# The last pair of heads in layer A: queries, keys and values turned by VectorE and moved through DRAM, and layer A's output product in another order of tiles

## The chip, the core and the metric

The kernel runs on one core of a Trainium2 chip. A core has five engines with instruction streams of their own: TensorE (PE) multiplies matrices into PSUM, which has eight banks; VectorE (DVE), ScalarE (ACT) and GpSimd (POOL) work elementwise; SyncE (SP) issues the DMAs of this kernel. They are ordered only by semaphores. The metric is the time of one execution on the device in microseconds (us), the median of several.

## The reference

Two layers on 512 tokens of width 1024, all in float32. Layer A attends within dilated windows of three kinds, and merges the three by the denominators of their softmaxes. Layer B attends within neighbourhoods of a grid of 8 x 64 tokens. Cut to layer A:

```python
def mixer_a(hn, w_in, w_out, q_gain, k_gain, t5_bias):
    proj = hn @ w_in
    ...
    for g, (window, dilation) in enumerate(((128, 1), (512, 4), (2048, 16))):
        q = rms_norm(qkv[:, :, g, 0], q_gain[g])
        k = rms_norm(qkv[:, :, g, 1], k_gain[g])
        o, lse = dilated_group_attention(q, k, v, t5_bias[...], dilation, reach)
        ...
    alpha = jax.nn.softmax(jnp.stack(lses), axis=0)
    y = jnp.sum(alpha[..., None] * jnp.stack(outs), axis=0)
    y = y.reshape(b, s, BRANCH_WIDTH).astype(hn.dtype) * jax.nn.silu(gate)
    return y @ w_out

def reference(x, ...):
    for i in range(DEPTH):
        hn = rms_norm(x, norm_gain[i])
        y = mixer_a(hn, ...) if i % 2 == 0 else mixer_b(hn, ...)
        x = x + y
```

There are 16 heads of 64 columns. The kernel takes them as eight pairs (`hc` 0 to 7) of 128 columns.

## The kernel before

**Products.** A float32 operand is held as a high and a low part, and each product of two 128-wide tiles is three matmuls (`mm3`, line 243, recorded at line 237). `splits` (line 188) makes both parts of a weight: ScalarE casts the high part (line 141), VectorE or GpSimd subtracts it to get the low part (line 149). The weights come in pieces of at most 1024 columns (`wraw`, line 201), three pieces ahead of their use; of the halves made from them, up to four wait for PE.

**Stages of layer A.** For each pair `main_a` (line 661) runs the projection of keys of the far groups, their values, and queries with the near key (`project_qk`, keys `rawk` and `rawq`), 32 steps each, then the near values (`v0_a`) and the gate (`gate_a`), 8 steps each. For the last pair the order is: `rawq`, `rawk`, the gate of pair 6, values, gate. Behind it comes the output product (`out_product`, line 1126), in which eight tiles of 128 output columns are added up over the eight pairs' y. Its first four tiles go over pairs 0 to 6 (28 steps), then three more tiles over pairs 0 to 6 (21 steps), then all seven take pair 7, and the eighth tile goes over all pairs.

**Between the projections.** The side work of a pair is: norm of queries and keys (`head_norm`, scaled at line 335), scores and softmax (`attn_a`), turning of the probabilities, and their weighting of the values (`weigh`, then `put_y`). The scores need queries and keys with the head's columns on the partitions, so both have to be transposed. Pairs 0 to 6 do this without PE: VectorE turns blocks of 32 x 32 in place (`turn_raw`, line 588, recorded at 592), a DMA writes the whole tile of 1536 KB to DRAM (`qd`, line 722), four DMAs of 384 KB read the blocks back in the places they belong to (`qt`, line 729), and ScalarE copies them into four areas (`split_q`, lines 777 and 791). Near values take the same way (`move_v`: `vd`, `vv`, then a copy into `v0`), and so do the probabilities (`turner`: `td`, `pt`).

Pair 7 uses PE instead: `q_a` and `k_a` transpose six groups of four tiles of 128 x 128 by PE (`transpose4`, recorded at line 241) into PSUM, from where ScalarE and VectorE copy them (lines 705, 708, 712, 680); `v_a` does one such group with the values. Its probabilities are transposed by PE too, in eight groups (`turn_p`, line 1007); these are outside the change.

**What sets the order.** PE runs in the order in which the program emits its instructions. That order comes from a planner: `run` (line 1092) walks through the steps of `main` and, between them, through the `side` work. Its clock counts PE work in units of its own (`matmul`, line 233): three matmuls of 512 columns are 640 units, a transpose 109. `later_on(delay, job)` puts a job on this clock; `yield "wait", key, delay` puts the side work off until a stamp's time plus a delay; `yield 600` puts it off by that much; a bare `yield` by the next of a cycle (500, 500, 700 for the last pair). `yield key, "turned"` in the output product makes the main work wait until the side has set that stamp, and the planner then emits side work until it has. The other engines are ordered by a scheduler that works with a simulated timeline, except for instructions under `tc.keep_in_program_order`. All engines and the DMA issue on SP take their instructions strictly in that order, so a waiting one holds up those behind it.

**PSUM.** Four banks hold the tiles that are being added up (`acc`), four are shared by scores (four at a time), transposes, weighting (two) and the later tiles of the output product (`acc2`).

**Around the last pair before.** Its scores of the first half wait for the stamp of its own gate; they come two steps into the output product. The weighting of pair 6 follows, then transposes of probabilities, the second half's scores, their transposes, and the values' group. Only then "turned" is stamped and the last weighting is emitted, after the 28th step; three `acc2` tiles follow. The bias of a pair (`bias_a`, five DMAs) is loaded 26,000 units after the start of its projections.

Of the kernel before, what the change touches and what calls it, by code (L numbers as in the profile page):

```python
# [22 lines left out]
P = 128  # L23
# [9 lines left out]
LINE = 384 + 2 * 448  # L33
W5 = 5 * 32
RUN = 6 * 64
EB = 8 * W5

# [15 lines left out]
OUTS = {  # L53
    A_OUT: ((512, 7), (384, 7), (512, 1), (384, 1), (128, 8)),
    B_OUT: ((512, 6), (256, 6), (512, 1), (256, 1), (128, 7), (512, 1), (384, 1), (128, 8)),
# [4 lines left out]
def tile_hybrid_encoder(  # L60
# [457 lines left out]

    moved = lambda hc: hc < NHC - 1

    def part(n):
        return rk[:, 1024 * n : 1024 * n + 1024].rearrange("p (i c) -> p i c", i=4)

    def project_qk(n, ns, key, hc, guard, first=False, **kw):

        box = []
        blocked = key == "raw" or (moved(hc) and key in FS)

        def evac(i, acc):
            if not box:  # L530
                if blocked:
                    box.append(key)
                elif key == "rawk":
                    box.append(rq[:, 2048:3072].rearrange("p (i c) -> p i c", i=4))
                elif key == "v":
                    box.append(rk[:, 4 * n * hc : 4 * n * hc + 4 * n].rearrange("p (i c) -> p i c", i=4))
                else:
                    box.append(rq[:, : 4 * n].rearrange("p (i c) -> p i c", i=4))
                if key == "rawk":
                    st["v12", hc] = part(hc % 3)  # L540
                box.append(None if key == "v" else wk.tile([P, 32], F32, tag="ss", name="ss"))
            raw, ss = box
            if blocked:
# [12 lines left out]
            if not first and key != "v":  # L556
                v = blocks_of(i, key + "0" * (key == "raw")) if blocked else raw[:, i, : ns * 64]
                squares(v, ss, i, ns, key == "rawq" and moved(hc))

# [22 lines left out]
    def normed(raw, ss, ns, key, hc):  # L582
        delay = 11000 if key == "rawk" and 0 < hc < NHC - 1 else 0
        head_norm(raw, ss, ns, delay, key == "rawk" and hc == NHC - 1, then=partial(turn_raw, key) if moved(hc) else None)
        st[key, hc] = raw
        stamp[key, hc] = clock[0]
# [36 lines left out]
    def v0_a(hc):  # L623
        acc = []
        yield from project_t(acc)
        yield "v", hc - 1
        vt = vv[:, :S]
        rows = lambda t, a, b: trj(t)[:, a:b]
        for a, b, to in ((0, 28, 4), (28, 32, 0)):
            src = to_trj(acc[0])[:, a:b]  # L630
            nc.vector.tensor_mul(rows(vt, to, to + b - a), src, rows(rs_half, a, b))
        if hc < NHC - 1:
            move_v(hc, vt)
        st["vt", hc] = vt
        stamp["vt", hc] = clock[0]
# [36 lines left out]

    def k_a(hc):
        yield "wait", ("rawk", hc), 12000
        qt = q_tiles(hc)[0]
        raw = st.pop(("rawk", hc))
        for g in range(2):
            tp = transpose4(raw, g * P)
            dst = qt[:, :, 4 + g, :].rearrange("p t (j r) -> p t j r", j=4)
            nc.vector.tensor_scalar(dst, to_tjr(tp), gk[:, g + 1 : g + 2], None, op0=ALU.mult)  # L680
            yield

    def q_tiles(hc):
# [9 lines left out]
    def q_a(hc):  # L693

        yield "wait", ("rawq", hc), 8000 if moved(hc) else 30500
        raw = st.pop(("rawq", hc))
        if moved(hc):
            move_q(hc)
            return
        qt, k0 = q_tiles(hc)  # L700

        by_t = lambda to: qt[:, :, to, :].rearrange("p t (x r) -> p x t r", x=16)
        of_t = lambda tp: tp.rearrange("p (x t r) -> p x t r", x=16, t=4)
        tp = transpose4(raw, 0)
        nc.scalar.copy(by_t(0), of_t(tp))
        yield
        tp = transpose4(raw, 3 * P)
        scaled(trj(k0[:, 64:EXT]), to_trj(tp), 0)
        yield
        for g in range(2):  # L710
            tp = transpose4(raw, (g + 1) * P)
            nc.vector.tensor_copy(by_t(1 + g), of_t(tp))
            yield
        stamp["q", hc] = 0

    def move_q(hc):
# [17 lines left out]
        def land():  # L734
            for a in (0, 2, 1, 3):
                later_on(6500 if hc < NHC - 2 else 5000, partial(read, a))
            yield "wait", ("rawk" if hc < NHC - 2 else "rawq", hc + 1), 0
            assert not left[0]
            split_q(hc, *q_tiles(hc))
            yield  # L740
# [27 lines left out]
    def split_q(hc, qt, k0):  # L768
# [3 lines left out]
        both = slot(hc, "q12", F32)  # L772
        areas = st["areas", hc] = slot(KT - 1, "q0", F32)[:, :S], both[:, :S], both[:, S:]
        for g, to in enumerate(areas):
            src = qt[:, :, g, :].rearrange("p s (x r) -> p s x r", r=8)
            dst = to.rearrange("p (x s r) -> p s x r", s=4, r=8)
            tc.keep_in_program_order(scaled(dst, src, g) if g else nc.scalar.copy(dst, src))

    def v_a(hc):

        yield "wait", ("vt", hc), 2500
        vt = st.pop(("vt", hc))
        tp = bank("tp")
        for i in range(4):
            transpose(tp[:, i * P : (i + 1) * P], vt[:, i * P : (i + 1) * P])
        nc.scalar.mul(v0[hc % 2], tp.rearrange("p (i c) -> p i c", i=4), 2.0)
        stamp["v", hc] = 0
        yield

# [142 lines left out]
    def attn_a(hc):  # L932
# [192 lines left out]

    def out_product(key, sink, late, more):

# [45 lines left out]
        if more == 3:  # L1173
            for k in range(KT):
                yield from step(k, (7,))
            return
# [159 lines left out]
    def main():  # L1336
        for hc in range(NHC):
            if hc:
                later_on(26000, lambda hc=hc: st.__setitem__(("e", hc), bias_a(hc)))
            yield from main_a(hc)  # L1340
        yield from out_product("ya", sink_a, 1, 3)
        gap[0] = cycle((500, 500, 800))
# [8 lines left out]
        for kind, i in B_PARTS:  # L1351
# [4 lines left out]
            else:  # L1356
                yield from gate_b(i)
        yield from out_product("yb", sink_b, 2, 2)

    def side():  # L1360
# [22 lines left out]
        for hc in range(NHC):  # L1383
# [84 lines left out]
def _layout(x, norm_gain, a_w_in, a_w_out, a_q_gain, a_k_gain, t5_bias,  # L1468
# [5 lines left out]

    def outs(w, late, more):
        k, m = KT - late, 512 + P * more
        blk = [w[:k, :, :512], w[:k, :, 512:m]]
        if more == 2:
            blk += [w[k : k + 1, :, :512], w[k : k + 1, :, 512:m], w[: KT - 1, :, 768:896]]
        blk += [w[KT - 1 :, :, :512], w[KT - 1 :, :, 512:896], w[:, :, 896:]]  # L1480
        return [b.transpose(1, 0, 2).reshape(P, -1) for b in blk]
# [6 lines left out]
    for hc in range(NHC):  # L1488
# [4 lines left out]
        parts.append(cols(wa, [9 * D + P * hc]))  # L1493
    parts += outs(wao, 1, 3)
    for kind, i in B_PARTS:
# [6 lines left out]
        parts.append(cols(wb, starts))  # L1502
    parts += outs(wbo, 2, 2)
    w = np.concatenate(parts, axis=1)
# [35 lines left out]
```

## Time and profile before

| | us |
|---|---|
| median of 3 runs | 800.97 |
| lowest, highest | 800.83, 800.97 |
| the profiled execution | 802.38 |
| its span, first to last instruction | 800.6 |
| busy: PE, DVE, ACT, POOL | 795.9, 526.8, 442.3, 222.2 |

The granted clock of TensorE is 1.00 throughout. The durations used below come from the one profiled execution, whose own time is 1.4 us above the median of the runs; between its span and its time lie 1.8 us. In the tables a row names the source line, the engine, the operation, and output<-inputs by the names of tiles; `x` is the count.

### The profile page before, as it was taken

The page shows a single profiled execution, that of the slowest core. Times are in us where ns is not written, and L with a number is a line of the kernel's source. Part 1 is how long each engine was busy: PE and PEld are TensorE (multiplying, and loading weights), DVE is VectorE, ACT ScalarE, POOL GpSimd, SP SyncE. Part 2 cuts the span into 40 slices and gives each one's busy share as a digit, 9 for nine tenths or more (in the row PEclk, how much of TensorE's full clock was granted, in tenths as well). Part 3 has the DMA queues.
Part 4 walks back from the last instruction along what each step waited for, and adds up shares of the span by engine and source line. Part 5 has one row for each costly group of instructions (what it writes and reads, how often), then busy time and mean ns, then how long its engine had stood idle before and what let it go on. Part 6 is the DMA issues. An engine that isn't in the chain of part 4 may idle for free.

```text
span 800.6 us, 17757 instructions
## 1 busy us (share of the span) xinstructions
PE 795.9 (99%) x6718; PEld 653.9 (82%) x6718; DVE 526.8 (66%) x1409; ACT 442.3 (55%) x933; POOL 222.2 (28%) x351
## 2 busy tenths in 40 slices
PE   9999999999999999999999999999999999999998
PEld 7888888888888888888888878888888888887887
DVE  7474575677577467568468568538655878896744
ACT  7442744745744754654664575636336666656721
POOL 2242532441432532432432331211220305020010
PEclk9999999999999999999999999999999999999999
DMA  8578587877977976986987966166646796899464
GB/s 293 159 206 260 162 246 213 262 204 228 297 219 212 280 236 206 275 289 198 264 259 232 267 201 186 31 208 214 167 151 202 204 245 213 207 263 292 147 156 175
DMA packets 97526, 174.76 MB, mean 218 GB/s; under 512 B 16608, under 2 KB 52592, under 8 KB 97440
## 3 DMA queue, kind: packets, MB, share of 16 engines
q1 hardware_dynamic: 97296, 173.36, 74.4%
q8 instruction: 53, 0.87, 0.5%
q14 instruction: 33, 0.27, 0.1%
q10 hardware_dynamic: 144, 0.26, 0.1%
HBM read 130.98 MB, written 50.86 MB: 227 GB/s over the span
## 4 chain that ended last, share of the span: by engine, by line
PE 90%; DVE 5%; DMA 3%; ACT 2%; issue 1%; ACTq 0%; SPq 0%
PE acc L237 79%; PE log L237 4%; PE o L237 4%; DMA vv<-vd 1%; DVE rawq L335 1%; DMA bd<-rawq 1%; PE tp L241 1%; DVE wl L149 1%; DMA wraw<-in_w 1%; PE busy L401 1%; ACT wh L141 0%; ACT p L1300 0%; DVE na L128 0%; ACT p L1305 0%; DVE rawq L592 0%
## 5 line engine op out<-in xcount | busy, mean ns | idle before, releaser
L237 PE MATMUL acc<-wh,hn_h 128*128 128x512 f32 x704 | 277.5, 395 | 0.0
L237 PE MATMUL acc<-wl,hn_h 128*128 128x512 f32 x704 | 273.7, 389 | 0.0
L237 PE MATMUL acc<-wh,hn_l 128*128 128x512 f32 x704 | 273.7, 389 | 0.0
L141 ACT CAST wh<-wraw 128x512 fp32r<-128x512 f32 (+1 forms) x258 | 157.7, 614 | 196.6 <-PE acc L237 168.4
L149 DVE TENSOR_TENSOR wl<-wraw,wh 128x512 fp32r<-128x512 f32 (+2 forms) x187 | 137.6, 737 | 151.4 <-ACT wh L141 149.6
L149 POOL TENSOR_TENSOR wl<-wraw,wh 128x512 fp32r<-128x512 f32 (+1 forms) x72 | 96.3, 1338 | 230.0 <-ACT wh L141 176.4
L237 PEld LDWEIGHTS acc<-wh,hn_h 128*128 128x128 f32 x704 | 132.4, 188 | 31.5 <-issue 3.8
L237 PEld LDWEIGHTS acc<-wh,hn_l 128*128 128x128 f32 x704 | 132.1, 188 | 27.9
L237 PEld LDWEIGHTS acc<-wl,hn_h 128*128 128x128 f32 x704 | 132.2, 188 | 26.8 <-POOL wl L149 0.3
L315 POOL TENSOR_TENSOR sq<-rawq 128x256 f32<-128x256 f32 (+1 forms) x82 | 59.4, 733 | 125.4 <-ACT rawq L555 112.7
L237 PE MATMUL acc<-y,wh 128*128 128x512 f32 (+1 forms) x272 | 81.5, 383 | 0.0
L1003 ACT ACTIVATE p<-p,mn 128x512 f32<-128x512 f32 (+1 forms) x64 | 44.8, 701 | 59.9 <-DVE mn L992 59.9
L237 PE MATMUL acc<-hn_h,wh 128*128 128x512 f32 x192 | 75.9, 395 | 0.1
L237 PE MATMUL acc<-hn_h,wl 128*128 128x512 f32 x192 | 74.8, 390 | 0.0
L237 PE MATMUL acc<-hn_l,wh 128*128 128x512 f32 x192 | 74.8, 390 | 0.0
L316 DVE TENSOR_REDUCE ss<-sq 128x4 f32<-128x256 f32 (+1 forms) x96 | 47.6, 506 | 32.5 <-POOL sq L315 32.1
L237 PEld LDWEIGHTS acc<-y,wh 128*128 128x128 f32 x272 | 48.8, 188 | 9.2 <-issue 0.7
L237 PE MATMUL acc<-y,wl 128*128 128x512 f32 (+1 forms) x136 | 51.4, 378 | 0.0
L335 DVE TENSOR_TENSOR rawq<-rawq,rs 128x256 f32<-128x256 f32 (+1 forms) x96 | 47.0, 550 | 2.5 <-POOL rs L133 2.2
L911 DVE STREAM_TRANSPOSE tr<-p 128x512 f32<-128x512 f32 x56 | 38.9, 706 | 11.6 <-ACT p L827 11.4
L555 ACT ACTIVATE rawq<-acc,rs_n 128x512 f32<-128x512 f32 (+1 forms) x76 | 46.1, 613 | 0.5
L827 ACT ACTIVATE p<-p,mn 128x512 f32<-128x512 f32 (+1 forms) x64 | 44.3, 700 | 2.1 <-DVE mn L826 2.1
(140 smaller groups left out, 907.5 us busy)
## 6 DMA issues: line engine op xcount, KB each, us to landing
wraw<-in_w SPq DMA_DIRECT2D x120, 512.0 KB, 5.5
td<-tr SPq DMA_DIRECT2D x14, 1024.0 KB, 7.2
pt<-td SPq DMA_DIRECT2D x56, 256.0 KB, 4.7
qd<-rawq SPq DMA_DIRECT2D x7, 1536.0 KB, 7.6
qt<-qd SPq DMA_DIRECT2D x28, 384.0 KB, 6.7
tdb<-tb SPq DMA_DIRECT2D x8, 768.0 KB, 5.6
pt<-tdb SPq DMA_DIRECT2D x32, 192.0 KB, 6.1
eb<-eb_d SPq DMA_DIRECT2D x32, 160.0 KB, 4.9
```

The lines of the kernel that those rows point to most:

```text
L141: nc.scalar.copy(h, raw)
L149: eng.tensor_sub(l, raw, h.bitcast(F32))
L237: nc.tensor.matmul(o, l, r, **kw)
L241: nc.tensor.transpose(o, i, ident)
L315: nc.gpsimd.tensor_mul(to, v, v)
L316: nc.vector.tensor_reduce(ss[:, i * ns : (i + 1) * ns], sq.rearrange("p (a b) -> p a b", b=64), axis=AX.X, op=ALU.add)
L335: m = nc.vector.tensor_mul(v, v, by)
L401: nc.tensor.matmul(busy, wide(P), wide(S), start=True, stop=True)
L555: nc.scalar.activation(dst, src, AF.Copy, scale=rs_n[:, i : i + 1])
L827: nc.scalar.activation(pr, pr, AF.Copy, scale=mn[:, 3:4])
L911: nc.vector.transpose(dst, src[:, :n].rearrange(order, b=4, k=32, **({"g": 2} if apart else {})))
L1003: nc.scalar.activation(row, row, AF.Exp, bias=mn[:, 1:2], scale=-1.0, accum_out=mn[:, 2:3])
```

## The change

The last pair goes the way of the others: VectorE turns its queries, keys and values, and they move through DRAM. `k_a` and `v_a` are gone, and so are the PE transposes of `q_a`. The write waits for the keys' stamp and `Q7` units, the split for 10,000 units more, and the first scores for 3,500 after that. As the y tile of pair 7 is now used for pair 7's own areas, the area of the near queries moves into a free part of `rawk`'s tile. The last pair's bias is loaded later.

In the output product of layer A the second phase has two `acc2` tiles instead of three. It starts at the stamp "turned", which is now set behind the scores of the second half; the third tile follows behind the stamp "last", which is set behind the last weighting. The layout of the weights in DRAM follows this order.

```diff
+Q7 = 9500
...
-    A_OUT: ((512, 7), (384, 7), (512, 1), (384, 1), (128, 8)),
+    A_OUT: ((512, 7), (256, 7), (128, 7), (512, 1), (384, 1), (128, 8)),
...
-        blocked = key == "raw" or (moved(hc) and key in FS)
+        blocked = key == "raw" or key in FS
...
-                squares(v, ss, i, ns, key == "rawq" and moved(hc))
+                squares(v, ss, i, ns, key == "rawq")
...
-        head_norm(raw, ss, ns, delay, key == "rawk" and hc == NHC - 1, then=partial(turn_raw, key) if moved(hc) else None)
+        head_norm(raw, ss, ns, delay, key == "rawk" and hc == NHC - 1, then=partial(turn_raw, key))
...
-        if hc < NHC - 1:
-            move_v(hc, vt)
-        st["vt", hc] = vt
+        move_v(hc, vt)
...
-    def k_a(hc):
...
-        yield "wait", ("rawq", hc), 8000 if moved(hc) else 30500
...
+        yield "wait", *((("rawq", hc), 8000) if hc < NHC - 1 else (("rawk", hc), Q7))
+        del st["rawq", hc]
+        move_q(hc)
...
-            yield "wait", ("rawk" if hc < NHC - 2 else "rawq", hc + 1), 0
+            if hc < NHC - 1:
+                yield "wait", ("rawk" if hc < NHC - 2 else "rawq", hc + 1), 0
+            else:
+                yield "wait", ("rawk", hc), Q7 + 10000
...
-        areas = st["areas", hc] = slot(KT - 1, "q0", F32)[:, :S], both[:, :S], both[:, S:]
+        areas = st["areas", hc] = rk[:, 3072 : 3072 + S], both[:, :S], both[:, S:]
...
-    def v_a(hc):
...
-                if u == 0:
-                    yield "wait", ("gate", hc), 500
-                yield 600
+                yield 3500 if u == 0 else 600
                 held = scores(u)
+                if u:
+                    stamp["ya", "turned"] = 0
                 yield 3200
...
-            yield from v_a(hc)
-            stamp["ya", "turned"] = 0
+            yield "wait", ("v", hc), 0
             put_y(hc, weigh(), True, True)
+            stamp["ya", "last"] = 0
             yield
...
         yield key, "turned"
-        for f in range(4, 4 + more):
+        for f in range(4, 6):
             acc[f] = bank("acc2")
         for k in range(KT - late):
-            yield from step(k, range(4, 4 + more))
-        if more == 2:
+            yield from step(k, range(4, 6))
+        if late == 2:
             k = KT - late
             yield key, k, "y"
             yield from step(k, range(4))
             yield from step(k, range(4, 6))
-            yield key, "last"
-            acc[6] = bank("acc2")
-            for k in range(KT - 1):
-                yield from step(k, (6,))
+        yield key, "last"
+        acc[6] = bank("acc2")
+        for k in range(KT - 1):
+            yield from step(k, (6,))
         yield key, KT - 1, "y"
...
-                later_on(26000, lambda hc=hc: st.__setitem__(("e", hc), bias_a(hc)))
+                later_on(26000 if hc < NHC - 1 else 44000, lambda hc=hc: st.__setitem__(("e", hc), bias_a(hc)))
...
-                yield from chain(q_a(hc), k_a(hc))
+                yield from q_a(hc)
+                yield from st.pop(("land", hc))()
                 yield from attn_a(hc)
```

More of the change, by code (lines that the diff above doesn't have):

```diff
@@ L517, in by_a @@
         return rq[:, : 512 * fs].rearrange("p (a x) -> p a x", a=4)[:, :, P * f0 : P * f1]
-    moved = lambda hc: hc < NHC - 1
     def part(n):
@@ L671, in main_a @@
             yield from gate_a(hc)
-    def k_a(hc):
[L674 to L681, printed above, removed]
     def q_tiles(hc):
@@ L693, in q_a @@
     def q_a(hc):
-        yield "wait", ("rawq", hc), 8000 if moved(hc) else 30500
[L696 to L714, printed above, removed]
+        yield "wait", *((("rawq", hc), 8000) if hc < NHC - 1 else (("rawk", hc), Q7))
+        del st["rawq", hc]
+        move_q(hc)
     def move_q(hc):
@@ L777, in split_q @@
             tc.keep_in_program_order(scaled(dst, src, g) if g else nc.scalar.copy(dst, src))
-    def v_a(hc):
[L781 to L788, printed above, removed]
     def scaled(dst, src, g):
@@ L1124, in tile_hybrid_encoder, with out_product @@
     gap = [cycle((1200,))]
-    def out_product(key, sink, late, more):
+    def out_product(key, sink, late):
         acc = {}
@@ L1172, in out_product @@
         acc[7] = ps_acc.tile([P, 512], F32, tag="acc", name="acc")
-        if more == 3:
+        if late == 1:
             for k in range(KT):
@@ L1338, in main @@
             if hc:
-                later_on(26000, lambda hc=hc: st.__setitem__(("e", hc), bias_a(hc)))
+                later_on(26000 if hc < NHC - 1 else 44000, lambda hc=hc: st.__setitem__(("e", hc), bias_a(hc)))
             yield from main_a(hc)
-        yield from out_product("ya", sink_a, 1, 3)
+        yield from out_product("ya", sink_a, 1)
         gap[0] = cycle((500, 500, 800))
@@ L1357, in main @@
                 yield from gate_b(i)
-        yield from out_product("yb", sink_b, 2, 2)
+        yield from out_product("yb", sink_b, 2)
     def side():
@@ L1473, in _layout, with outs @@
     wb, wbo = f(b_w_in)[0].reshape(KT, P, -1), f(b_w_out)[0].reshape(KT, P, D)
[L1475 to L1480, printed above, removed]
+    def outs(w, late):
+        k = KT - late
+        blk = [w[:k, :, :512], w[:k, :, 512:768]]
+        if late == 2:
+            blk += [w[k : k + 1, :, :512], w[k : k + 1, :, 512:768]]
+        blk += [w[: KT - 1, :, 768:896], w[KT - 1 :, :, :512], w[KT - 1 :, :, 512:896], w[:, :, 896:]]
         return [b.transpose(1, 0, 2).reshape(P, -1) for b in blk]
@@ L1493, in _layout @@
         parts.append(cols(wa, [9 * D + P * hc]))
-    parts += outs(wao, 1, 3)
+    parts += outs(wao, 1)
     for kind, i in B_PARTS:
@@ L1502, in _layout @@
         parts.append(cols(wb, starts))
-    parts += outs(wbo, 2, 2)
+    parts += outs(wbo, 2)
     w = np.concatenate(parts, axis=1)
```

## The prediction

> **What bounds the kernel now.** I read the page first: the busy times and the shares of the chain that ended last.
>
> ```profile
> span 800.6 us, 17757 instructions
> PE 795.9 (99%) x6718; PEld 653.9 (82%) x6718; DVE 526.8 (66%) x1409; ACT 442.3 (55%) x933; POOL 222.2 (28%) x351
> PE 90%; DVE 5%; DMA 3%; ACT 2%; issue 1%; ACTq 0%; SPq 0%
> ```
>
> TensorE is busy for 795.9 of 800.6 us. A busy PE need not be PE at its peak, so I looked next at what PE waited for over the whole span.
>
> ```profile
> PE busy L401 <- DVE warm L390: 0.9, 1, 0.9
> PE o L237 <- DVE mn L826: 0.6, 1, 0.6
> ```
>
> There are two waits in 800 us, and 0.9 of the 1.5 us is the start. So every microsecond of PE work taken out shortens the program, and every new wait of PE lengthens it by its own size: there is no idle time for a wait to hide in. The third view is the chain in order of time (start, length, what, count) around the last pair. It runs on PE without a break, so it also serves as PE's timetable.
>
> ```profile
> 473.28 6.35 PE acc L237 x27
> 479.63 0.44 PE tp L241 x4
> ...
> 489.86 5.47 PE acc L237 x24
> 495.33 1.84 PE log L237 x96
> 497.17 4.31 PE acc L237 x18
> 501.49 2.72 PE o L237 x120
> ...
> 523.10 0.44 PE tp L241 x4
> ```
>
> Three products make one step of the planner: 24 in 5.47 us are eight steps, 0.684 us each. The first row holds the last 2 steps of the last pair's key projection and 7 of the gate that follows, so the projection ends at 473.28 + 2 x 0.684 = 474.65. I call this instant K. The group of four transposes at 479.63 is the first of seven that the change removes, and that at 523.10 the last. The scores of the first half stand at 495.33, two steps into the output product.
>
> **What is removed from PE.** The forms of the transposes, in the groups of instructions:
>
> ```profile
> L241 PE MATMUL tp<-ident,rawq 128*128 128x128 f32 x24 | 3.6, 272 | 0.0
> L241 PE MATMUL tp<-ident,vv 128*128 128x128 f32 x4 | 0.6, 272 | 0.0
> ```
>
> Busy time would make this 4.2 us, but matmuls overlap; in the timetable a group of four takes 0.44. Seven groups (four for queries and the near key, two for far keys, one for values) are 7 x 0.44 = **-3.1 us**, bounds -3.1 and -4.2. All of it is on the path, since PE has no gaps. By the Trainium skill (VectorE: DVE Perf Modes, The three transpose paths) a TensorE transpose of 128x128 bf16 takes 390 ns, which for 28 would be an estimated 10.9 us saved; the 0.11 us each of this trace (f32) decides. The same page (Rules for kernel authors) gives a whole 128x128 transpose to TensorE where a PSUM destination will do. That speaks against this change; the next parts price it.
>
> **The old wait.** The 0.6 us is put down to VectorE, but the weighting also reads probabilities that come back from DRAM:
>
> ```profile
> 454.75 0.30 SPq L924 DMA_DIRECT2D pt<-td  x1
> pt<-td SPq DMA_DIRECT2D x1, 256.0 KB, 8.7
> ```
>
> 454.75 + 8.7 = 463.4, and PE goes on at 463.63. Ahead of these reads stand the last pair's bias loads, which the change moves from 26,000 to 44,000 units after that pair's start, behind them. I count **-0.6 us**. The added VectorE turn of 2.37 us (shown below) lands at about 460, ahead of that pair's softmax; at the worst it hands PE the 2.4 us as a wait in place of the 0.6. So: -0.6 to +1.8. Both K and what follows from it move alike.
>
> **What takes its place: the last pair's queries and keys.** This is the term that decides. When PE comes to the scores follows from the planner's clock, where a step is 3 x 512 / 2.4 = 640 units. From K, gate, values and gate are 24 steps without transposes. The write is due at K + 9500 and 600 on top: step 16. The reads come 5000 after the resuming at step 15: step 23. The four copies of the split are due at K + 19500: step 31 (19,840). Then 500 and 3500: the scores follow step 38 (24,320), 14 steps into the output product instead of two. On the chip that is 474.65 + 38 x 0.684 = **500.6**.
>
> When the data are there is read from VectorE's timeline and from the earlier pairs, which go this way already:
>
> ```profile
> 485.00 0.68 DVE L712 COPY qt<-tp 128x512 f32<-128x512 f32 x1
> 485.60 0.68 DVE L613 TENSOR_TENSOR gt<-gt,rs_half 128x512 f32<-128x512 f32 x1
> 486.61 1.43 DVE L335 TENSOR_TENSOR rawq<-rawq,rs 128x256 f32<-128x256 f32 x4
> 407.36 1.30 DVE L592 STREAM_TRANSPOSE rawq<-rawq 128x512 f32<-128x512 f32 x2
> 427.36 2.37 DVE L592 STREAM_TRANSPOSE rawq<-rawq 128x1024 f32<-128x1024 f32 x2
> 456.27 3.59 DVE L335 TENSOR_TENSOR rawq<-rawq,rs 128x512 f32<-128x512 f32 x4
> ```
>
> The keys are scaled (L335) until 488.04. The copy L712 ahead of them goes (-0.6 with its overlap), and their turn of 1.30 is added: turned at 488.7. If the gate's L613 falls behind them too, 488.1. The queries' turn (2.37) follows their scaling, which ends at 459.9 in the last row; that is 28 us before, and hidden but for the bound above. The DMA issue on SP is in order: the write, due at step 16 (485.6), waits there for 3 us with weight loads behind it. Those are several halves of a piece ahead, a half lasts four steps (2.7 us), so I count nothing; without that cover it would be up to 3 us.
>
> ```profile
> L722 SPq DMA_DIRECT2D qd<-rawq x1: 377/377/377, 429.8 to 429.8; - x1
> qd<-rawq SPq DMA_DIRECT2D x1, 1536.0 KB, 5.4
> L729 SPq DMA_DIRECT2D qt<-qd x4: 303/424/432, 131.2 to 132.5; - x4
> DMA to landing us min/median/max: 3.9/6.6/7.8
> ...
> L729 SPq DMA_DIRECT2D qt<-qd x4: 303/424/1764, 377.4 to 378.7; - x4
> L722 SPq DMA_DIRECT2D qd<-rawq x1: 382/382/382, 369.8 to 369.8; - x1
> DMA to landing us min/median/max: 5.2/7.6/9.5
> ```
>
> The fastest write is that of pair 6, 5.4 us. The reads can't be issued before it has landed. The four reads of pair 1 go from 131.2 to 132.5 + 7.8 = 140.3: 9.1 us. Together 14.5. Pair 5 needs from 369.8 to 378.7 + 9.5 = 388.2: 18.4. I take 14.5, since the queues are quieter here than there:
>
> ```profile
> 488.00:497.00 9.00, 9.00 (x133) 7.36 (x131) 6.11 (x16) 2.45 (x5) 1.59 (x2) 1.00 0.76 211
> 497.00:505.00 8.00, 8.00 (x154) 6.64 (x143) 4.04 (x19) 6.79 (x15) 1.28 (x1) 1.00 0.08 28
> ```
>
> The last two columns are the DMA share and GB/s. Hence 488.7 + 14.5 = 503.2. Then ScalarE splits, as for pair 6:
>
> ```profile
> 447.55 1.26 ACT L791 ACTIVATE k<-qt,gk 128x512 f32<-128x512 f32 x1 [1.32 <-DMA qt<-qd]
> 448.69 0.62 ACT L777 COPY q<-qt 128x512 f32<-128x512 f32 x1
> 449.20 1.35 ACT L791 ACTIVATE q<-qt,gk 128x512 f32<-128x512 f32 x2
> ```
>
> 3.0 us for the four copies: 506.3. Scores of the first group can start after two of them; the third group, at about 0.55 us into the 1.84, needs the last. So the scores run as if begun at 505.8, against 500.6: a new wait of **+5.2 us**. With 18.4 for the transfer it is 9.1. For the other end, let each read land the 3.9 of the fastest one after its own issue: 1.3 + 3.9 = 5.2, with the write 10.6, a wait of 1.3. By the Trainium skill (DMA: Bandwidth & Descriptors, Anatomy of one DMA) a transfer takes an estimated 2.0 us and its bytes at 436 GB/s: 5.6 for the write, which the 5.4 here bears out, and 5.6 for the reads in one stream, which the 9.1 here does not; by it the wait would be 1.9.
>
> While ScalarE waits for the landing, the weight casts behind the split wait too. PE has four halves ready, 11 us of steps, and waits itself: nothing.
>
> **Smaller terms.** The weighting of pair 6 comes 5 steps after the scores. Its y is first used in the 25th step of the output product: 5 steps and 4 groups of transposes later, 3.4 + 1.8 = 5.2 us.
>
> ```profile
> 506.31 1.12 ACT L864 CAST y<-gt 128x512 fp32r<-128x512 f32 x1 [1.48 <-DVE gt L857]
> 507.51 1.57 POOL L867 TENSOR_TENSOR y<-gt,y 128x512 fp32r<-128x512 f32 x1 [3.65 <-ACT y L864]
> 529.14 1.33 DVE L850 TENSOR_TENSOR y<-gt,y 128x128 fp32r<-128x128 f32 x4
> ```
>
> In the trace y is whole at 509.1, 4.9 us after the weighting's end (504.2); the softmax and held-back casts on ScalarE may add 1.5. Two banks of PSUM for the second half's transposes instead of four can cost some tenths. Together **+0.5**, bounds 0 and +1.5. The last weighting now has 12 steps (8.2 us) before its y is used, instead of 21; it was whole at 530.5, 3.5 after the weighting's end at 526.9. Values go through DRAM from step 29 on and are placed about 15 steps before the last weighting. The regrouped weight slices carry the same products: nothing.
>
> **Sum.** -3.1 - 0.6 + 5.2 + 0.5 = +2.0. The profiled execution would go from a span of 800.6 to 802.6, and with the 1.8 us around it from 802.4 to 804.4. The runs shown have a median of 800.97, 1.4 below it; the difference carries over: **803.0 us**.
>
> **The rivals.**
> - *The reads overlap* (the other side). The queues are nearly idle from 497 on (0.08), so the four reads may land as calculated for the lower end. That decides where the transfer falls below 12.4 us: then the wait of 3.1 is no more than what the transposes gave. At 10.6: -3.1 - 0.6 + 1.3 + 0.5 = -1.9, 799.1; with the wait wholly hidden 797.3. Against it: none of seven pairs was under 14.5 by its best parts.
> - *Break-even.* The keys are turned at 488.1 or earlier and one or two us of the transfer go: wait 2.5 to 4, time 800.3 to 801.8.
> - *The long transfer.* The write, with probabilities' reads and a blocked weight load on the same in-order SP, takes 18.4 as for pair 5, and y of pair 6 is late by 1.5 on top: -3.7 + 9.1 + 1.5 = +6.9, 807.9; half way 805.5. For it: five of the seven writes are well above 5.4 (up to 8); against it the idle queues.
> - *It doesn't do what it says*: the planner puts the scores later than step 38, with the same effect as the first rival.
>
> **Chances.** Forecast (801.8 to 804.8) 0.44; reads overlap or scores planned later (below 799.4) 0.24; break-even 0.18; long transfer 0.14. Some 0.2% (1.6 us) is what a measurement tells from no change: faster 0.24, same 0.27 (break-even and the forecast's lower edge), slower 0.49. The range leaves out little of the outer cases: 797.6 to 806.0.
>
> **What would show it.** Right: only 32 transposes on PE, the wait on L826 gone, and one new wait of 4 to 6 us at the scores of the last pair, released by ScalarE's split, that itself waits for DMA into qt until about 503. Wrong: qt landed by 498, or the split idle for less than 2 us, or PE waiting at y of pair 6 instead.

## The result, and the profile after

The changed kernel takes 814.16 us (median; 813.76 to 815.16), the kernel before 800.97 beside it: ratio 1.0166, interval 1.0149 to 1.0184. It is slower by 13.2 us, 1.65%. The profiled execution took 815.16 with a span of 813.4, against a span of 800.6 before.

The page of the changed kernel, busy times and the shares of the last chain:

```profile
span 813.4 us, 17707 instructions
PE 795.8 (98%) x6690; PEld 652.2 (80%) x6690; DVE 531.3 (65%) x1409; ACT 444.4 (55%) x936; POOL 221.2 (27%) x349
PE 82%; DVE 8%; DMA 5%; ACT 2%; issue 1%; POOL 0%; SPq 0%; ACTq 0%; DVEq 0%; POOLq 0%
```

The 28 transposes are gone (6718 to 6690 instructions), yet PE's busy time is the same, 795.8 against 795.9: something else got longer. DMA has risen from 3% to 5% of the chain. What PE waited for:

```profile
PE log L238 <- ACT rawk L750: 12.5, 1, 12.5
PE busy L402 <- DVE warm L391: 0.9, 1, 0.9
PE acc L238 <- DVE mn L954: 0.6, 1, 0.6
PE acc L238 <- POOL y L829: 0.4, 1, 0.4
```

One wait of 12.5 us, at the scores (`log`) of the last pair, put down to ScalarE's split. (The two kernels' line numbers differ: products are recorded at line 238 here and 237 before, the scaling at 336 and 335, VectorE's turn at 591 and 592; the split's rows are L750 and L753 instead of L777 and L791.) The row names only the last releaser; the chain in order of time (start, length, what) says what ScalarE stood for:

```profile
487.81 1.09 DVE rawq L336 x3
...
489.42 1.30 DVE rawq L591 x2
...
491.72 7.93 DMA qd<-rawq
...
501.02 9.57 DMA qt<-qd
...
510.70 1.18 ACT k L753
511.87 0.52 ACT rawk L750
...
512.43 3.63 PE log L238 x96
516.06 5.44 PE acc L238 x18
```

The keys are turned at 490.72 (489.42 + 1.30), the write lands at 499.65, the last of the four reads at 510.59: 19.9 us from turn to landing. The scores then take 3.63 us and the six steps behind them 5.44, against 1.84 and 4.31 before. The table of stretches (start:end, length, busy us of PE, PEld, DVE, ACT, POOL, then PE's granted clock, DMA share, GB/s) shows why:

```profile
491.00:500.00 9.00, 8.94 (x40) 7.02 (x38) 6.32 (x11) 2.66 (x5) 3.02 (x3) 1.00 0.87 295
500.00:511.00 11.00, 0.00 (x0) 0.00 (x0) 0.00 (x0) 0.30 (x1) 0.00 (x0) 0.72 1.04 237
511.00:514.00 3.00, 1.57 (x48) 0.89 (x56) 0.00 (x0) 2.62 (x4) 0.00 (x0) 0.50 1.11 262
514.00:518.00 4.00, 4.00 (x69) 2.83 (x54) 2.65 (x15) 2.48 (x6) 0.00 (x0) 0.50 0.27 90
518.00:521.00 3.00, 3.00 (x14) 2.43 (x13) 1.26 (x7) 2.81 (x8) 0.03 (x1) 0.93 0.00 0
```

During the wait the granted clock falls (1.00 until 504, 0.50 from 505 on), and PE comes back to work at 0.50: scores and steps lose 1.8 + 1.1 = 2.9 us. The balance: -3.1 (transposes) + 12.5 (the wait) + 2.9 (the clock) + 1.0 (the two small waits) = +13.3, against 13.2 between the medians. The old wait of 0.6 has no part in it; the medians of before seem not to hold it, as is worked out further below.

The same stretches also show DMA at 1.04: the transfer ran with the 16 engines full. The DMA view from the write's issue to the last landing, 40 slices:

```profile
DMA  0939999999999997999889999999999999999999
...
DMA packets 2363, 5.16 MB, mean 273 GB/s; under 512 B 171, under 2 KB 683, under 8 KB 2362
```

In these 18.9 us 5.16 MB move. The pair's own write and reads are 2 x 1536 KB = 3.1 MB of it; the rest, 2.0 MB, is weights, probabilities and values. While the write runs (491.72 to 499.65) 315 GB/s are moved at a share of 0.94; while the reads run (499.65 to 510.59) it is 243 GB/s at 1.04. The full engines move less while the reads run. Next, the same 20 us before and after:

```profile
494.00:514.00 20.00, 20.00 (x378) 16.29 (x378) 12.57 (x41) 10.74 (x22) 3.09 (x4) 1.00 0.23 68
```

```profile
494.00:514.00 20.00, 7.50 (x75) 5.47 (x81) 3.32 (x5) 5.20 (x8) 1.29 (x1) 0.77 1.05 282
```

68 GB/s over 20 us are 1.4 MB, 282 are 5.6 MB. In the 18.9 us from 491.72 on the kernel before moved 1.68 MB, near the 2.0 MB that here are not the transfer's own. The quiet stretch that the prediction relied on was quiet because the pair's 3.1 MB weren't moved there; the change fills it.

### The profile page after: what moved, and what is told of

The parts are those of the page before. It is cut to its first block, busy times and chain, and to the rows that moved or that the text cites. A ratio compares the mean times of both kernels' runs of the same rounds, so it can differ in the third digit from the quotient of the medians.

```text
span 813.4 us, 17707 instructions
## 1 busy us (share of the span) xinstructions
PE 795.8 (98%) x6690; PEld 652.2 (80%) x6690; DVE 531.3 (65%) x1409; ACT 444.4 (55%) x936; POOL 221.2 (27%) x349
## 4 chain that ended last, share of the span: by engine, by line
PE 82%; DVE 8%; DMA 5%; ACT 2%; issue 1%; POOL 0%; SPq 0%; ACTq 0%; DVEq 0%; POOLq 0%
PE acc L238 73%; PE log L238 4%; PE o L238 4%; DMA wraw<-in_w 2%; DVE wl L150 1%; DVE rawq L336 1%; DMA qt<-qd 1%; DMA vv<-vd 1%; DMA qd<-rawq 1%; DMA vv<-bd 1%; DVE rawq L591 1%; PE busy L402 1%; DVE p L942 1%; ACT p L1262 0%; DVE na L129 0%
## 5 line engine op out<-in xcount | busy, mean ns | idle before, releaser
L316 POOL TENSOR_TENSOR sq<-rawq 128x256 f32<-128x256 f32 (+1 forms) x80 | 57.7, 729 | 123.4 <-ACT rawq L554 109.8
```

The costliest lines, as they stand in the source:

```text
L316: nc.gpsimd.tensor_mul(to, v, v)
```

## The experiments

What stands under "Theory" and "Rival" is the text on record from before each run. Times are compared with runs of the kernel before on the same chip.

**What of the change is free.** First the new order of tiles alone, on the kernel before:

```diff
-    A_OUT: ((512, 7), (384, 7), (512, 1), (384, 1), (128, 8)),
+    A_OUT: ((512, 7), (256, 7), (128, 7), (512, 1), (384, 1), (128, 8)),
...
+                if u:
+                    stamp["ya", "turned"] = 0
```

> The kernel before with the new order of layer A's output product alone (two late tiles from the stamp 'turned' on, the third behind 'last'); queries, keys and values of the last pair still go through PE. Theory (the loss is the new wait of PE for the scores of the last pair, 12.5 us, and what the wait does to the clock): no loss from the order of tiles, 800.4 to 801.8 us, no PE wait above 0.7 us. Rival (the order of tiles, with two shared PSUM banks for the last transposes and other weight pieces, costs a part of the 13 us): 803 or more, with PE waits after the scores of the second half.

Measured: 801.42 against 801.18, ratio 1.0 (0.999 to 1.0009), and PE waits for nothing but the start (0.9). The order of tiles costs nothing. Note that the 0.6 us wait on L826, which stands in the profile of before, is missing here too, though no load was moved.

Then the values alone, through DRAM, with the late bias:

```diff
-        if hc < NHC - 1:
-            move_v(hc, vt)
+        move_v(hc, vt)
...
-            yield from v_a(hc)
+            yield "wait", ("v", hc), 0
```

> The kernel before, with the last pair's values alone turned by VectorE and moved through DRAM, and its bias loaded at 44,000 units; queries and keys by PE, old order of tiles. Theory (a part whose transfer has time to land costs PE nothing): one group of transposes (0.44 us) and the old wait (0.6 to 1.0 us) go, no new PE wait: 799.3 to 800.3. Rival (the added DMAs of 0.5 MB or VectorE's turn push something late): 801 or more.

Measured: 800.96 against 801.22, ratio 0.9996 (0.9986 to 1.0006). That is above the expected range. The four transposes it spares are 0.44 us, too little to tell from no change here, and the old wait isn't gained either. Its profile has one new PE wait, 0.9 us for ScalarE's `hn_h` (L425) at the start of layer B, which was not expected. In any case the loss doesn't come from the values.

**The cold clock.** 50 matmuls that compute nothing used, put in front of the last pair's scores, keep PE busy while it would wait:

```diff
+                if u == 0:
+                    warmer = bank("busy")
+                    for _ in range(50):
+                        nc.tensor.matmul(warmer, wide(P), wide(S), start=True, stop=True)
```

> The changed kernel with 50 matmuls of ones (128x512, results unused) on PE ahead of the last pair's scores, so that PE works for some 11 of the 12.5 us of the wait. Theory (after the wait PE runs at a lower granted clock: the scores took 3.63 us against 1.84, the next six steps 5.44 against 4.32): the scores begin at the same 512.4, take 1.8 to 2.0 us, the granted clock stays at 1.00, the time falls by 2.5 to 3.2 us to about 811.3. Rival (they are slow because operands or banks come late): 814, scores still above 3 us.

Measured: 812.15 (one run), 2.0 less than the changed kernel. The rows of the chain in this run:

```profile
511.47 1.25 ACT q L753 x2
...
512.77 1.37 PE log L238 x64
514.13 4.30 PE acc L238 x18
```

The granted clock stays at 1.00, and the six steps are back at 4.30. The scores begin at 511.52, 0.9 earlier than in the changed kernel, and with the six steps they take 6.9 us against 9.1. So some 2 us of the loss are the clock, less than was expected: at full clock the scores stand for the last areas of ScalarE's split (L753), which the slow scores of the changed kernel hide. The Trainium skill (TensorE: Matmul & The Clock Gate, Part 1: The HAM clock gate) says that after an idle window of some 3.4 us TensorE runs at half clock until it has been busy for about as long. Here the granted clock of 0.50 until 518, some 5.6 us after the scores' start, agrees in kind; it lasts longer.

**Is it the turn that is late, or the transfer that is long?** The keys' turn is later than predicted since the queries' turn now sits in front of pair 6's softmax. Moving it 17,000 units later:

```diff
-        delay = 11000 if key == "rawk" and 0 < hc < NHC - 1 else 0
+        delay = 11000 if key == "rawk" and 0 < hc < NHC - 1 else 17000 if key == "rawq" and hc == NHC - 1 else 0
```

> The changed kernel with the scaling and turn of the last pair's queries put 17,000 units later, behind the softmax of pair 6's first half instead of into it. Theory (the turn of 2.4 us in the middle of that softmax makes VectorE and ScalarE late for the keys, which were turned 17.1 us after the key projection's end instead of 14.1): keys turned 1.5 to 3 us earlier, time lower by as much, 811 to 812.7. Rival (the keys are late for another reason, or the write waits on SP anyway): within 0.7 of 814.

Measured: 816.11 (one run). The chain:

```profile
487.38 1.20 DVE rawq L591 x2
...
488.59 9.62 DMA qd<-rawq
...
499.60 11.57 DMA qt<-qd
```

This is above both cases. The keys are turned 2.1 us earlier and the write is issued 3.1 earlier (488.59 against 491.72), but the last read lands at 511.17, 0.6 later. Write and reads are 1.7 and 2.0 longer, together more than was gained: from the write's issue to the last landing 6.38 MB move here, 5.16 MB in the changed kernel. The turn is indeed late because of the queries' turn, but in this run an earlier one didn't bring the keys earlier.

The bias loads (1 MB), back at 26,000 units:

```diff
-                later_on(26000 if hc < NHC - 1 else 44000, lambda hc=hc: st.__setitem__(("e", hc), bias_a(hc)))
+                later_on(26000, lambda hc=hc: st.__setitem__(("e", hc), bias_a(hc)))
```

> The changed kernel with the last pair's bias loaded 26,000 units after the pair's start again, as before the change. Theory (the later load is what took away the old wait of pair 5's weighting; it stands too far ahead of the last pair's transfer to shift its landing): the wait of 0.5 to 1 us at that weighting is back, the wait at the last scores stays 12 to 13 us; 814.5 to 815.3. Rival (the bias loads are part of the traffic that makes the last transfer late): the wait at the last scores falls by 2 to 3 us, 811.5 to 812.5.

Measured: 814.31 (one run), wait 11.8. Neither case came: the time is that of the changed kernel, the wait 0.7 less, and no wait comes back at pair 5's weighting. The loss doesn't hang on the bias, and nothing here shows that its loads had caused the old wait.

Everything of the last pair later, `Q7 = 14500`, so that more steps stand ahead of the scores:

```diff
-Q7 = 9500
+Q7 = 14500
```

> The changed kernel with Q7 = 14500 in place of 9500: split and scores of the last pair stand about 7 steps (4.8 us) later in PE's order, the write to DRAM is due later too, though not later than the turn ends. Theory (the wait is data's arrival less PE's arrival): the wait at the scores falls by 4 to 5.5 us to 7 to 8.5; but the weighting of pair 6 is then forced right ahead of the first use of its y, which costs a second wait of 3 to 5 us: 812 to 815. Rival (the transfer starts later by as much, so the wait moves along): wait 11 to 13 us, 817 or more.

Measured: 819.12 (one run). The time is as the rival has it (817 or more), the wait of 9.3 lies between the two. PE's waits in that run:

```profile
PE log L238 <- ACT rawk L750: 9.3, 1, 9.3
PE acc L238 <- ACT y L826: 4.6, 1, 4.6
PE acc L238 <- POOL y L829: 1.1, 1, 1.1
```

The wait at the scores falls by 3.2 and not by 4 or more, since the last read lands at 512.34, 1.7 later; and pair 6's y, which hangs on its weighting behind these scores, is now late by 4.6 + 1.1 = 5.7 us. There is no room behind the scores for a delay.

**Fewer bytes behind the last turn.** Only the two far groups of keys depend on the last projection. Here the queries and the near key (1 MB) go earlier in a transfer of their own, and the far keys (0.5 MB, once out and once back) are left for the end:

```diff
+        if ahead:
+            write, read, _ = mover(hc, 0, 4)
+            later_on(18000, write)
+            for a in (0, 2, 1, 3):
+                later_on(25500, partial(read, a))
...
+        write, read, left = mover(hc, 4, 6)
```

> The changed kernel, but the last pair's queries and near key (1024 KB) are written and read back some 17 us ahead of its far keys, and only the far keys (512 KB) take the way through DRAM behind their turn; the split by ScalarE comes ahead of it. Planner's place of the scores unchanged. Theory (the wait is the length of the transfer behind the turn: 1536 KB out and back on one queue at some 235 GB/s with weight pieces between): of 19.9 us from turn to landing some 9 to 12 are left, the split falls out of the path, the wait falls from 12.5 to 0 to 4 us, the clock stays up; 798 to 803 us. Rival (the wait is set by the late turn and by SP's order, not by bytes): the wait stays above 8 us, 808 or more.

Measured: 805.42 against 801.18, ratio 1.0049 (1.0032 to 1.0066). Waits and chain:

```profile
PE acc L238 <- ACT wh L142: 2.0, 1, 2.0
PE log L238 <- DMA qt<-qd: 0.9, 2, 0.6
```

```profile
496.23 3.86 DMA qd<-rawq
...
501.46 3.85 DMA qt<-qd
```

A third of the bytes need 9.1 us from issue to landing in place of 18.9, and the wait at the scores falls to 0.9. Two thirds of the loss are gone. The time is 2.4 above the theory's range: there is a new wait of 2.0 for weights, and the granted clock falls behind it, to a mean of 0.72 from 494 to 500. With the early transfer the engines are full from 474 to 494.

```profile
474.00:484.00 10.00, 10.00 (x46) 8.29 (x45) 8.38 (x32) 8.86 (x20) 3.38 (x6) 1.00 1.06 243
484.00:494.00 10.00, 8.03 (x36) 6.32 (x34) 6.55 (x17) 4.63 (x8) 0.74 (x1) 1.00 1.05 286
```

So the same with the bias at 57,000 units:

```diff
-                later_on(26000 if hc < NHC - 1 else 44000, lambda hc=hc: st.__setitem__(("e", hc), bias_a(hc)))
+                later_on(26000 if hc < NHC - 1 else 57000, lambda hc=hc: st.__setitem__(("e", hc), bias_a(hc)))
```

> As the run that sent the queries and nearest keys ahead and only the far keys (0.5 MB) after the last turn, which took 805.4; here the last pair's bias loads move from 44,000 to 57,000 units, so that their 1 MB leaves the queue's full stretch from 474 to 494 us. Theory (the queue's bytes set what lands when): the weights land in time, the 2.0 wait for them at layer A's output and its low clock go, the far keys' last read lands at 500 to 503, the wait at the scores is 0 to 3, time 797.5 to 801. Rival (the round trip itself, write 3.9 and reads 5.2 after a turn at about 491, and not the bytes ahead of it, sets the end): the keys land at 504 to 506 as before, time 803 to 806. A third outcome: the biases come too late and PE waits for the first weighting of the last pair; then a wait there and the scores on time.

Measured: 802.47 against 801.25, ratio 1.0024 (1.0013 to 1.0035).

```profile
492.19 6.09 DMA qd<-rawq
...
499.65 2.98 DMA qt<-qd
...
PE log L238 <- DMA qt<-qd: 2.3, 2, 2.0
```

The weights are in time, the keys land at 502.63 and the wait is 2.3, all as the theory had it; the time is 1.5 above its range, of which two waits that the changed kernel has too (0.6 at a softmax, 0.4 at pair 6's y) explain a part; no row accounts for the rest. Two of the seven executions took 803.88 and 805.88, as long as the rival has it. Behind this wait, of which 2.0 us are in one piece, the granted clock stays at 1.00; behind the 2.0 us of the run before it fell. So no length of wait can be named here below which the clock holds. Even 0.5 MB out and back between the last projection and its scores isn't hidden.

**One queue, or the engines behind it?** The write is issued by ScalarE and the reads by GpSimd, so that neither stands behind SyncE's weights:

```diff
-            tc.keep_in_program_order(nc.sync.dma_start(d.rearrange("a p x -> p a x"), rq.rearrange("p (a x) -> p a x", a=4)))
+            by = nc.scalar if hc == NHC - 1 else nc.sync
+            tc.keep_in_program_order(by.dma_start(d.rearrange("a p x -> p a x"), rq.rearrange("p (a x) -> p a x", a=4)))
...
-            tc.keep_in_program_order(nc.sync.dma_start(dst, src))
+            by = nc.gpsimd if hc == NHC - 1 else nc.sync
+            tc.keep_in_program_order(by.dma_start(dst, src))
```

> As the changed kernel, but the last pair's write (1.5 MB) is issued by ScalarE and its four reads by GpSimd, so that neither stands in SyncE's queue behind weights, values and probabilities. In the changed kernel the write took 7.9 us and the reads 10.9, 19.9 us from the end of the last turn to the last landing, and PE waited 12.5. Theory A (the order within SyncE's one queue: the pieces issued ahead of the reads, 1.5 MB between 492 and 494, go first): the way falls to 14 to 16 us, the wait to 6 to 9, time 807 to 811. Theory B (the 16 engines' bandwidth is full, share 1.0 at some 235 GB/s, whoever issued first): the way stays 18 to 20 us, the wait 11 to 13, time 812 to 815. A cost that could hide a gain: GpSimd stands at its reads until the write has landed, and its low half of the weights waits behind them; if so, a wait of PE on wl before the scores of about 1 to 3 us.

Measured: 816.41 (two runs) against 801.4, wait 14.8.

```profile
490.43 8.30 DMA qd<-rawq
...
500.86 11.90 DMA qt<-qd
```

From turn to landing 22.4 us, longer even than theory B had: SyncE, no longer held up by the write, sends all four reads of probabilities and the weights ahead of the pair's reads, and they share the engines with the transfer. With the write alone on ScalarE and the reads on SyncE:

> As the run before it, but only the write is issued by ScalarE; the reads stay on SyncE behind the weights and values. Theory A (order within SyncE's queue): the write lands in 5 to 6 us after its issue instead of 7.9, the reads as in the changed kernel (10.9); way 17 to 18 us, wait 10 to 11, time 811 to 813. Theory B (bandwidth of the engines): the write takes 7.5 to 8.5, the wait 12 to 13, time 813 to 815.

```profile
489.93 8.46 DMA qd<-rawq
...
499.77 9.70 DMA qt<-qd
```

Measured: 813.73 (two runs), wait 11.8, write 8.46: the write and the time are as theory B has them, the wait lies between the two. The place in the queue doesn't help; what is full is the engines. From the write's issue to the last landing the four runs moved:

| run | MB | us | GB/s |
|---|---|---|---|
| the changed kernel | 5.16 | 18.9 | 273 |
| queries' turn later | 6.38 | 22.6 | 283 |
| write on ScalarE, reads on GpSimd | 6.10 | 22.3 | 273 |
| write on ScalarE alone | 5.30 | 19.5 | 271 |

The rate hardly changes; the time goes with the bytes. The Trainium skill says of the queues (DMA: Bandwidth & Descriptors, Issuing engines are not separate DMA queues) that DMAs of the scalar, sync and gpsimd engines run on the same 16 DMA engines and interleave, whoever started them. Both runs agree.

**A version that keeps the gain.** Queries, near key and values go by VectorE and DRAM, early; the far keys, which are projected last, stay with PE (two groups of transposes). A first one:

```diff
+    def k_a(hc):
+        yield "wait", ("rawk", hc), 15500
+        qt = q_tiles(hc)[0]
+        raw = st.pop(("rawk", hc))
+        for g in range(2):
+            tp = transpose4(raw, g * P)
+            dst = qt[:, :, 4 + g, :].rearrange("p t (j r) -> p t j r", j=4)
+            nc.vector.tensor_scalar(dst, to_tjr(tp), gk[:, g + 1 : g + 2], None, op0=ALU.mult)
+            yield
...
+            split_q(hc, *q_tiles(hc))
+            yield
+            yield from k_a(hc)
```

> The changed kernel with the last pair's queries and near key through DRAM some 17 us early (as in the run with the keys apart), its far keys transposed by PE (two groups, 0.9 us), the split at 9,500 units behind the key projection, the bias at 57,000 units, behind these transfers; values through DRAM, new order of tiles. Theory (only the far keys came too late for a transfer; the weights that were late with the keys apart are on time once the bias loads are out of that stretch): no PE wait above 1 us, clock 1.00; 797 to 799.5. Rival (the 1 MB of queries in the busiest stretch of the queue makes weights or probabilities late): PE waits of 2 us or more on weights, 801 or more.

Measured: 799.16 against 801.22, ratio 0.9975 (0.9966 to 0.9985). Here the far keys carry a gain that the queries carry already, so it counts twice, and this kernel doesn't compute the layer; its time alone is used here. The next one only copies them:

```diff
-            nc.vector.tensor_scalar(dst, to_tjr(tp), gk[:, g + 1 : g + 2], None, op0=ALU.mult)
+            nc.vector.tensor_copy(dst, to_tjr(tp))
```

> The last pair's queries, nearest keys and values go by VectorE and DRAM as in the changed kernel, the queries' part of the transfer early, and the two far groups of keys are transposed by TensorE as in the kernel before, here only copied out of the bank, since the queries already carry the gains. Theory (the change loses at the round trip of the keys that are projected last, all else of it is about free): no wait over 1 us at the last pair's scores, five groups of transposes fewer than before, time 798.7 to 800.0, ratio 0.997 to 0.9985 against before. Rival (the transposes that go from PE's way were hidden behind another limit, so nothing is won whatever is late): 800.6 to 801.6, and a new wait or a lower granted clock in the last pair. The copy out of the bank by another operation than before may shift this by 0.1 either way.

Measured: **798.94** (798.8 to 799.14) against 801.25, ratio 0.9972 (0.9961 to 0.9982): faster than both kernels by 2.3 and some 15 us. Its chain:

```profile
490.54 0.44 PE tp L242 x4
...
491.67 0.44 PE tp L242 x4
492.11 7.51 PE acc L238 x33
499.62 1.84 PE log L238 x96
501.46 4.31 PE acc L238 x18
```

The scores come at full clock and without a wait. Five groups are saved, 5 x 0.44 = 2.2 us, and 2.3 were measured: a transpose taken off PE is worth its length as long as nothing waits for what replaces it.

## Why the prediction was wrong in its size

The side was right (slower), and so was the place: 12.5 us at the last pair's scores, released by a split that waits for DMA into qt. The time, 814.2, lies far above the range. Step by step:

- **Transposes, -3.1: right.** Not seen alone in the changed kernel, but 2.2 by timetable came out as 2.3 for five of the seven groups.
- **The old wait, -0.6: right in the profile, wrong in its reason.** The wait is gone and the key projection ends 1.0 us earlier, as the first product of the gate shows, before and after:

```profile
474.71 0.39 PE L237 MATMUL acc<-hn_h,wh 128*128 128x512 f32 x1
```

```profile
473.70 0.39 PE L238 MATMUL acc<-hn_h,wh 128*128 128x512 f32 x1
```

  But it is missing as well with the tiles' order alone, and with the bias loads back at their place. The same first product of the gate starts between 473.3 and 473.8 in all thirteen other profiles, also with the order of tiles alone (473.63) and with the values alone (473.64). So the wait seems to belong to the one profiled execution of before, which was 1.4 us over its median; it should not have been in the sum.
- **PE at the scores at 500.6: right.** 512.43 - 12.5 = 499.9.
- **The new wait, +5.2: mis-sized, 12.5.** The 7.3 between them are: PE 0.7 earlier; the keys turned at 490.7 instead of 488.7 (2.0); the write issued 1.0 behind the turn instead of at once; the transfer 18.9 instead of 14.5 (4.4); and 0.8 back, since at half clock the scores needn't stand for the last areas of the split. The step that failed is the length of the transfer in this term, "I take 14.5, since the queues are quieter here than there": it measured 18.9. The 0.08 was the share of a kernel that didn't move the pair's bytes there, and it holds from 497 on; the row above it, 211 GB/s from 488 to 497, is 1.9 MB in the stretch into which the write falls. And the 14.5 was put together from the write of pair 6 and the reads of pair 1, which no pair had together. The rows of pair 6 in the trace of before, read as one transfer:

```profile
L729 SPq DMA_DIRECT2D qt<-qd x4: 324/427/431, 435.3 to 436.6; - x4
L722 SPq DMA_DIRECT2D qd<-rawq x1: 377/377/377, 429.8 to 429.8; - x1
...
DMA to landing us min/median/max: 5.4/7.5/10.8
```

  From 429.8 to 436.6 + 10.8 = 447.4 are 17.6 us: the fast write was followed by slow reads. Pair 1, with the fast reads, has a slow write ahead of them:

```profile
L722 SPq DMA_DIRECT2D qd<-rawq x1: 385/385/385, 123.4 to 123.4; - x1
```

  From 123.4 to the 140.3 of the prediction are 16.9. Read as wholes in this way, all seven pairs take 16.8 to 18.4, close to the 18.9 measured here; with 17.6 the prediction's own sum would have had a wait of 8.3.
- **"Hidden but for the bound above", the queries' turn: right in the end, for another reason.** It came at 461 ahead of pair 6's softmax and made the keys' turn late; but with it moved away the keys landed no earlier. By that run the 2.0 and the 4.4 above are not independent: the earlier start was spent in the transfer.
- **"The write waits on SP ... nothing": nearly.** 1.0 us behind a read of probabilities. Between the write and its reads SP issued 896 KB of weights and 256 KB of values, which the prediction didn't count; what of the transfer's length is theirs, no run separates.
- **The clock: put at nothing without a reason.** The prediction let a wait of 5.2 us cost 5.2. Here the wait cost 2.0 more by the run that kept PE warm, and 2.9 by the lengths in the chain, 0.8 of which full-clock scores would have stood for the split.
- **Smaller terms, +0.5: 1.0**, within the bounds (0.6 at a softmax, 0.4 at pair 6's y). The weighting of pair 6 comes six steps after the scores, as the x18 of the prediction's own chain says, and not five; so its y has less time than the 5.2 us counted.

The miss adds up: 7.3 at the wait, 2.9 at the clock, 0.6 of the old wait and 0.5 of the smaller terms are 11.3, against 11.2 between 803.0 and 814.2.

Of the rivals, the long transfer named the mechanism and the place. Its price, 807.9 at most, lacked the late turn and the clock. "The reads overlap" was refuted: four reads issued within 1.3 us landed one by one, the last 9.57 after its issue (shortest 5.6, median 7.6). The estimate after the Trainium skill (DMA: Bandwidth & Descriptors, Anatomy of one DMA), 5.6 for the write and 5.6 for the reads, gives 11.2 for the transfer; the 18.9 measured through full engines don't bear it out. The section gives this fit for single DMAs issued through GpSimd, while these are issued by SyncE.

Not settled: how much of the 18.9 us would remain on empty engines, since no run emptied them. Pair 1 of the kernel before comes near for the reads. In the 2.6 us ahead of them the share is 0.10, and while they run it is:

```profile
131.20:140.30 9.10, 9.10 (x42) 7.54 (x41) 2.36 (x4) 3.33 (x7) 2.58 (x2) 1.00 0.92 215
```

215 GB/s over 9.1 us are 1.95 MB, and 1.57 MB of it are the four reads themselves. So the reads fill the engines almost alone, at a lower rate than a write. With the fastest write, 5.4, this gives an estimated 14.5 for engines with little else to do. The prediction's figure was then about the best case, and the 4.4 us above it (2.5 in the write, 1.8 in the reads) would be the price of the other 2.0 MB.

## What to carry to other kernels

Take the length of a transfer whole from one occurrence, not its parts from several, and before calling a stretch of DMA free add to it the bytes that the change itself moves there. Work that can be done ahead may take the long way through DRAM, while the last product before its use should take the short one on TensorE: splitting the two was faster here than either alone. A wait of PE on the path can cost more than its own length: here 12.5 us of waiting brought some 2 us of slow restart.

## What was not expected of the hardware

Issuing from another engine's queue shortened nothing: the write took 8.30 and 8.46 us from ScalarE, 7.93 from SyncE. Starting a transfer 3.1 us earlier ended it 0.6 us later (one run). The reads filled the engines at some 215 to 243 GB/s, the write at 315. And PE's busy time didn't fall by the 3.1 us of transposes taken out, because the same instructions ran longer at a granted clock of 0.50; busy time alone would have hidden both. And a wait of 2.0 us was followed by a low clock in one run and not in another.
